# A hybrid decoder trunk on one core: the modulation vectors as row sums on VectorE, and h made one K-tile at a time

## The chip, the cores and the metric

One core of a Trainium2 chip. The metric is device time in microseconds (us) of one execution, the median over runs. Engines: TensorE (PE; its weight loads are PEld), VectorE (DVE), ScalarE (ACT), GpSimd (POOL), and SyncE (SP), on whose queue nearly all DMAs are issued.

## The reference

Two layers of a sub-layer of width 2048 over 512 tokens, batch 1. What matters here is how each layer begins and ends:

```python
c_act = jax.nn.silu(c)                                # (1, 2048)
for l in range(2):
    mod = c_act @ w_mod[l] + b_mod[l]                 # w_mod[l]: 2048 x 6144
    shift, scale, gate = jnp.split(mod, 3, axis=-1)
    h = rmsnorm(x, norm_gain[l]) * (1.0 + scale) + shift
    proj = h @ w_in[l]                                # 2048 x 7504, f32
    ...   # sparse attention with an indexer and top-k; chunked retention; SiLU gates
    x = x + gate * (y @ w_out[l])
```

`mod` is a matrix-vector product: 100 MB of `w_mod` in all, read once, for 12,288 numbers. Nothing of a layer's projection can begin before `shift` and `scale` of the first K-tile (128 of the 2048 columns) are known.

## The kernel before, in words

Everything is kept transposed: features on 128 partitions, 512 tokens along the row. There are 16 K-tiles of D = 2048. Each f32 operand of a large matmul is split into a high and a low fp32r part, and three products are summed. Weights stream through a ring of three buffers: `load_chunk` issues the DMA, `split_chunk` makes the high part on ACT (L268) and the low part on DVE (L269), `chunk_mm` issues the matmuls (L315 to L317 with weights stationary, L321 to L323 with h stationary).

**Modulation before.** A block of `w_mod` has rows of D on partitions. `mod_add` (L348, L350) multiplies it by the partition's entry of silu(c) and adds it into an accumulator on DVE. After 16 row blocks `mod_sum` (L333) sums over the partitions with matmuls against a column of ones, one per 128 columns, and `mod_put` (L338 to L344) adds bias and gain. For layer 0's shift and scale this is done in five phases of 2, 2, 4, 4, 4 K-tiles (`PH`). From the second phase on, the shift half is computed on PE instead (`mod0_pe`, L396, with `cz`), and summed in `mod0_sum` (L424). The rest (layer 0's gate, layer 1's three vectors) is done in `mod_rest`, a generator advanced at a rate per weight chunk (`MODN`).

**The start stage before.** `start()` runs with a schedule written by hand, in program order on every engine. It loads x (16 tiles) and the first blocks of `w_mod`, sums squares (L532 to L541) and makes rstd (L602, L515, L518). Then, phase by phase, it makes `shiftT` and `AT`, then h for the phase's K-tiles (`make_h0`, L550 to L556: two ACT activations and a DVE subtraction), then the matmul chunks that these K-tiles allow. Those are listed in `PLAN`: `S` is the group of keys, values and indexer keys (16 K-tiles in eight chunks, four PSUM tiles, 336 columns, evacuated by `evac_s`), and `("E", i, a, b)` is K-tiles a to b of an early part of one of eight column groups: indexer queries for i below 4 (finished later by the groups Q3), one head's q and k of the retention for i of 4 and above (finished later by the groups QK). An early part is kept in SBUF (L1191) or added to what is kept (L1206); `joined` (L1198) adds it at the end. Units of the bias table (`bias_tables`: indicators on ACT L740, matmuls L753, evacuation L756, a store) are put between chunks.

**After the start stage** the groups run in this order: Q3, VB, QK (four groups, each two heads of retention), QA, GA, GB, OUT; then layer 1. `step()` takes one chunk, and `fill` gives the pending tasks (indexer, top-k, rotary, retention, attention) a budget of 4 us of DVE work per chunk. `evac_qk` of one QK group and the retention tasks of the group before it share arena slots (A0 to A7).

The functions that the change touches, with the profile's line numbers:

Of the kernel before, what the change touches and what calls it, by code (L numbers as in the profile page):

```python
# [51 lines left out]
]  # L52
# [1229 lines left out]
```

## Time and profile before

| | |
|---|---|
| median of 3 runs | 1971.2 us (1970.82 to 1971.3) |
| profiled execution, its own time | 1972.98 us |
| its span, first to last instruction | 1971.2 us, mean granted TensorE clock 0.995 |
| busy share of PE, DVE, ACT | 98%, 65%, 42% |
| DMA | 304.44 MB, mean 154 GB/s |

How to read the lines: a group's row gives the kernel line, engine, operation, output tile <- input tiles, shapes and count, then busy us in all, the mean ns of one, and the engine's idle time just ahead of these instructions with what ended it. A timeline row gives start and duration in us, then the same names. A row of the chain gives start, duration and what ran. L515 and the like are lines of the kernel before. Matmuls overlap in a pipeline, so the distance from one start to the next is what a matmul costs TensorE, not its listed duration; an f32 matmul (L333, L396, L424, L515, L541) shows as two instructions. The granted clock is 1.00 at full speed.

### The profile page before, as it was taken

How to read it: one execution, taken by the hardware profiler on the slowest of the kernel's cores; microseconds unless marked ns; L12 is line 12 of the kernel's file. 1: busy time of each engine (PE TensorE's matmuls, PEld its weight loads, DVE VectorE, ACT ScalarE, POOL GpSimd, SP SyncE). 2: the span in 40 equal slices, each digit the busy share in tenths (PEclk: the TensorE clock that was granted, in tenths of full speed). 3: DMA queues.
4: the chain of work that ended last, by engine and by line, in shares of the span. 5: the costliest groups of instructions: out<-in, count | busy, mean ns of one | idle time of the engine just before them, and what ended most of it. 6: DMA issues, size and time to landing. Idle time of an engine off the chain costs nothing.

```text
span 1971.2 us, 25044 instructions
## 1 busy us (share of the span) xinstructions
PE 1933.8 (98%) x9384; PEld 1592.9 (81%) x9384; DVE 1271.5 (65%) x2126; ACT 822.4 (42%) x1500; POOL 3.6 (0%) x16
## 2 busy tenths in 40 slices
PE   6999999999999999999999999999999999999999
PEld 5677776788888888888889888888888888888887
DVE  5766999887658865766657459847666755233232
ACT  4554694354454642332225342234444564233111
POOL 0000000000000000000000000000000000000000
PEclk9999999999999999999999999999999999999999
DMA  9878644533334736768763222333332432333443
GB/s 330 301 246 272 231 151 145 165 101 103 96 113 141 238 113 229 258 229 299 260 204 108 86 85 75 106 101 93 97 107 86 129 118 65 96 97 118 139 139 106
DMA packets 170712, 304.44 MB, mean 154 GB/s; under 512 B 16736, under 2 KB 71008, under 8 KB 170592
## 3 DMA queue, kind: packets, MB, share of 16 engines
q1 hardware_dynamic: 170592, 302.86, 47.1%
q8 instruction: 73, 1.20, 0.2%
q14 instruction: 47, 0.39, 0.1%
HBM read 289.18 MB, written 13.63 MB: 154 GB/s over the span
## 4 chain that ended last, share of the span: by engine, by line
PE 85%; DVE 6%; ACT 4%; DMA 3%; issue 2%; SPq 0%; ACTq 0%; DVEq 0%
PE pj L315 19%; PE pj L317 19%; PE pj L316 19%; PE pj L321 5%; PE pj L323 5%; PE pj L322 5%; DVE wl L269 2%; DVE iacc L868 1%; DMA mw<-in_wmod_dram 1%; DVE m L867 1%; PE pdot L845 1%; DMA xT<-in_xt_dram 1%; PE pmod L396 1%; PE pm L333 1%; PE pdot L847 1%
## 5 line engine op out<-in xcount | busy, mean ns | idle before, releaser
L269 DVE TENSOR_TENSOR wl<-wf,wh 128x1024 fp32r<-128x1024 f32 (+2 forms) x308 | 366.1, 1189 | 440.7 <-ACT wh L268 427.7
L268 ACT ACTIVATE wh<-wf 128x1024 fp32r<-128x1024 f32 (+2 forms) x308 | 318.2, 1034 | 763.9 <-PE pj L316 552.1
L315 PE MATMUL pj<-h,wh 128*128 128x512 f32 x1280 | 504.4, 394 | 2.5 <-DVE vm L883 1.4
L316 PE MATMUL pj<-h,wh 128*128 128x512 f32 x1280 | 501.5, 392 | 0.0
L317 PE MATMUL pj<-h,wl 128*128 128x512 f32 x1280 | 501.4, 392 | 0.0
L315 PEld LDWEIGHTS pj<-h,wh 128*128 128x128 f32 x1280 | 241.6, 189 | 56.6 <-issue 3.7
L317 PEld LDWEIGHTS pj<-h,wl 128*128 128x128 f32 x1280 | 241.4, 189 | 50.6
L316 PEld LDWEIGHTS pj<-h,wh 128*128 128x128 f32 x1280 | 241.7, 189 | 48.7 <-issue 0.5
L321 PE MATMUL pj<-wh,h 128*128 128x512 f32 (+1 forms) x640 | 243.2, 380 | 3.4 <-ACT h L550 3.3
L323 PE MATMUL pj<-wh,h 128*128 128x512 f32 (+1 forms) x640 | 241.9, 379 | 1.8 <-DVE h L556 1.8
L322 PE MATMUL pj<-wl,h 128*128 128x512 f32 (+1 forms) x640 | 242.0, 378 | 0.0
L350 DVE SCALAR_TENSOR_TENSOR macc<-mw,cs,macc 128x1024 f32<-128x1024 f32 (+2 forms) x195 | 205.8, 1055 | 51.9 <-DMA mw<-in_wmod_dram 49.2
L315 PE MATMUL pj<-y,wh 128*128 128x512 f32 x512 | 199.6, 390 | 1.0 <-DVE xn L1163 1.0
L317 PE MATMUL pj<-y,wl 128*128 128x512 f32 x512 | 199.2, 389 | 0.0
L316 PE MATMUL pj<-y,wh 128*128 128x512 f32 x512 | 199.2, 389 | 0.0
L321 PEld LDWEIGHTS pj<-wh,h 128*128 128x128 f32 x640 | 121.4, 190 | 27.3 <-issue 4.3
L323 PEld LDWEIGHTS pj<-wh,h 128*128 128x128 f32 x640 | 121.2, 190 | 23.4 <-DVE h L556 2.7
L322 PEld LDWEIGHTS pj<-wl,h 128*128 128x128 f32 x640 | 121.5, 190 | 19.7 <-issue 0.8
L315 PEld LDWEIGHTS pj<-y,wh 128*128 128x128 f32 x512 | 96.1, 188 | 21.5 <-DVE xn L1163 1.4
L316 PEld LDWEIGHTS pj<-y,wh 128*128 128x128 f32 x512 | 96.1, 188 | 19.9
L317 PEld LDWEIGHTS pj<-y,wl 128*128 128x128 f32 x512 | 96.1, 188 | 19.9
L740 ACT ACTIVATE ind<-pos,pt 128x128 bf16<-128x128 f32 (+3 forms) x128 | 61.7, 558 | 0.1
(445 smaller groups left out, 2032.4 us busy)
## 6 DMA issues: line engine op xcount, KB each, us to landing
mw<-in_wmod_dram SPq DMA_DIRECT2D x192, 512.0 KB, 5.6
wf<-in_w_in_dram SPq DMA_DIRECT2D x152, 512.0 KB, 3.5
wf<-in_w_in_dram SPq DMA_DIRECT2D x148, 256.0 KB, 3.0
wf<-in_w_out_dram SPq DMA_DIRECT2D x64, 512.0 KB, 4.3
dec<-in_decay_dram SPq DMA_DIRECT2D x32, 256.0 KB, 4.0
xT<-in_xt_dram SPq DMA_DIRECT2D x16, 256.0 KB, 6.8
bias<-bias_d SPq DMA_DIRECT2D x16, 256.0 KB, 4.1
xr<-in_xt_dram SPq DMA_DIRECT2D x16, 256.0 KB, 5.5
```

What stands on the lines that cost most here:

```text
L268: act(h[:, :n], t[:, :n], AF.Copy)
L269: tt(lo[:, :n], t[:, :n], f(h[:, :n]), op=OP.subtract)
L315: mm(g.ps[n], wh[:, o:o + P], ah, start=s0, stop=False)
L316: mm(g.ps[n], wh[:, o:o + P], al, start=False, stop=False)
L317: mm(g.ps[n], wl[:, o:o + P], ah, start=False, stop=s1)
L321: mm(q, ah[:, n * P:(n + 1) * P], wh[:, o:o + g.N], start=s0, stop=False)
L322: mm(q, ah[:, n * P:(n + 1) * P], wl[:, o:o + g.N], start=False, stop=False)
L323: mm(q, al[:, n * P:(n + 1) * P], wh[:, o:o + g.N], start=False, stop=s1)
L333: mm(ps[:, j:j + 1], acc[:, j * P:(j + 1) * P], ones[:, :1], start=True, stop=True)
L350: stt(a, w, cs[:, rt:rt + 1], a, op0=OP.mult, op1=OP.add)
L396: mm(ps[32 * t:32 * t + 32, :wd], cz[:, 32 * (rt + u):32 * (rt + u) + 32], m0_tile[i][:, 2 * wd * u:2 * wd * u + wd], start=rnd == 0, stop ...
L740: act(v, pos[:, :w], AF.Sign, bias=pt[:, col:col + 1], scale=-1.0)
```

## The change

`w_mod` is laid out transposed by the host, in blocks of 128 columns of `mod` (on partitions) by 1024 rows of D. silu(c) is broadcast over the partitions once, as `cb`, by 16 matmuls against the identity and four ACT copies. Each block is one `tensor_tensor_reduce` on DVE: multiply by half of `cb` and sum along the row into one column, the second half starting from the first half's sum. `scale` is multiplied by the norm gain in the same instruction, and `mod_end` adds a prepared bias. The matmuls `mod_sum`, `mod0_sum` and `mod0_pe` are gone, with `cz`, the accumulators and the phases.

`start()` now makes h one K-tile at a time: four blocks of `w_mod` make shift and scale of a K-tile, and `make_h0` follows. A new `PLAN` lists the chunks, with some of them issued K-tile by K-tile; a modulation step (`mod_step`) is issued for every 2.0 us of matmul cost (`RMOD`), and one bias unit for every 6 us once three K-tiles are there. The plan holds 76 E K-tiles instead of 64: the early parts of the second QK group now reach K-tile 12 instead of 4, and those of the first Q3 group reach 6 instead of 8. High and low splits are issued separately, evacuations of a chunk after the modulation steps that follow it, and stores of the bias table after those. The load of the positions comes later. Beside the parts below, the diff moves the preparation of `pt` in `bias_tables` behind a `yield`, collects its stores in a queue, replaces `shiftT`, `AT` and `gateT` by `mod_col` wherever they are read, and builds `WORK` from `PLAN` (cost 1.36 per E K-tile, 1.85 per S K-tile).

```diff
-PH = [2, 2, 4, 4, 4]
-PK = [0, 2, 4, 8, 12, 16]
-PLAN = [
-    [("S", 0), ("E", 0, 0, 2), ("E", 1, 0, 2), ("E", 2, 0, 2), ("E", 3, 0, 2)],
-    [("S", 1), ("E", 4, 0, 4), ("E", 5, 0, 4), ("E", 6, 0, 4), ("E", 7, 0, 4)],
-    [("S", 2), ("S", 3), ("E", 0, 2, 8), ("E", 1, 2, 8), ("E", 2, 2, 8)],
-    [("S", 4), ("S", 5), ("E", 3, 2, 8), ("E", 4, 4, 12), ("E", 5, 4, 12)],
-    [("S", 6), ("S", 7)],
-]
-REST = [(0, 4), (0, 5), (1, 0), (1, 2), (1, 1), (1, 3), (1, 4), (1, 5)]
+PLAN = [("E", 0, 0, 2, 0), ("E", 1, 0, 2, 0), ("S", 0, 0), ("E", 0, 0, 2, 1), ("E", 1, 0, 2, 1), ("S", 0, 1),
+        ("E", 2, 0, 2), ("E", 3, 0, 2), ("E", 4, 0, 3), ("E", 5, 0, 3), ("S", 1), ("E", 6, 0, 4), ("E", 7, 0, 4),
+        ("E", 0, 2, 6), ("E", 1, 2, 6), ("S", 2), ("E", 2, 2, 8), ("E", 3, 2, 8), ("S", 3),
+        ("S", 4), ("E", 6, 4, 12), ("E", 7, 4, 12), ("S", 5), ("E", 4, 3, 12), ("E", 5, 3, 12), ("S", 6), ("S", 7)]
 NE = 8
-EARLY = [max(it[3] for p in PLAN for it in p if it[0] == "E" and it[1] == i) for i in range(NE)]
-ONPE = [False, True, True, True, True]
-NB0 = [0, 1, 1, 1, 1]
+EARLY = [max(it[3] for it in PLAN if it[0] == "E" and it[1] == i) for i in range(NE)]
+RMOD = 2.0
+RBIAS, KBIAS = 6.0, 3
+REST = [(0, 2, k) for k in range(16)] + [(1, q, k) for k in range(16) for q in (0, 1)] + [(1, 2, k) for k in range(16)]
 HVA = 2
-M0AHEAD = 7
+M0AHEAD = 8
 MX0 = 2
...
-    w = host["w_mod"]
-    mod = []
-    for p, n in enumerate(PH):
-        k = slice(P * PK[p], P * PK[p + 1])
-        mod.append(np.concatenate([w[0][:, :D][:, k], w[0][:, D:2 * D][:, k]], axis=1).ravel())
-    for l, b in REST:
-        mod.append(w[l][:, 2 * T * b:2 * T * (b + 1)].ravel())
+    seq = [(0, q, k) for k in range(KT) for q in (0, 1)] + REST
+    mod = np.stack([host["w_mod"][l][r * D // 2:(r + 1) * D // 2, q * D + P * k:q * D + P * (k + 1)].T
+                    for l, q, k in seq for r in range(2)])
     return {"xt": np.ascontiguousarray(host["x"].reshape(T, D).T), "positions": host["positions"].reshape(T),
-            "wmod": np.concatenate(mod), "w_in": host["w_in"], "w_out": host["w_out"],
...
-    cz = G("cz")
-    nc.vector.memset(cz, 0.0)
-    nc.vector.tensor_copy(cz.rearrange("p (k n) -> p k n", n=32)[:, :, 0:1], cs.unsqueeze(2))
     act(sm("dummy", 1), eps, AF.Sqrt)
+    cb = sm("cb", D)
+    for i in range(4):
+        ps = PX("pc")
+        for j in range(4):
+            n = 4 * i + j
+            mm(ps[:, j * P:(j + 1) * P], cs[:, n:n + 1].to_broadcast([P, P]), ident, start=True, stop=True)
+        act(cb[:, i * T:(i + 1) * T], ps, AF.Copy)
     gqk = [sm(f"gqk{l}", 1) for l in range(DEPTH)]
...
-    gateT = [sm(f"gate{l}", KT) for l in range(DEPTH)]
+    MD = [sm(f"md{l}", 3 * KT) for l in range(DEPTH)]
+    MB = [sm(f"mb{l}", 3 * KT) for l in range(DEPTH)]
+    for l in range(DEPTH):
+        b = MB[l][:, :2 * KT].rearrange("p (k a) -> p a k", a=2)
+        nc.vector.tensor_copy(b[:, 0], bm(l, 0, KT))
+        stt(b[:, 1], bm(l, KT, KT), 1.0, ng(l, 0, KT), op0=OP.add, op1=OP.mult)
+        nc.vector.tensor_copy(MB[l][:, 2 * KT:], bm(l, 2 * KT, KT))
+    def mod_col(l, q, k):
+        n = 2 * k + q if q < 2 else 2 * KT + k
+        return MD[l][:, n:n + 1]
...
+    def split_hi(i):
         g, ch = stream[i]
         n = g.kper * g.N
-        t = wf.pop(i)
         h = ring.tile([P, 1024], F32R, name="wh", tag="wh")
+        act(h[:, :n], wf[i][:, :n], AF.Copy)
+        whl[i] = h
+    def split_lo(i):
+        g, ch = stream[i]
+        n = g.kper * g.N
         lo = ring.tile([P, 1024], F32R, name="wl", tag="wl")
-        act(h[:, :n], t[:, :n], AF.Copy)
-        tt(lo[:, :n], t[:, :n], f(h[:, :n]), op=OP.subtract)
-        whl[i] = (h, lo)
-    def ahead(nd, ns):
+        tt(lo[:, :n], wf.pop(i)[:, :n], f(whl[i][:, :n]), op=OP.subtract)
+        whl[i] = (whl[i], lo)
+    def ahead(nd, ns, nh=0):
         while st["dma"] < min(nd, len(stream)):
             load_chunk(st["dma"])
             st["dma"] += 1
+        while st["hi"] < min(max(ns, nh), len(stream)):
+            split_hi(st["hi"])
+            st["hi"] += 1
+            if st["split"] < ns:
+                split_lo(st["split"])
+                st["split"] += 1
         while st["split"] < min(ns, len(stream)):
-            split_chunk(st["split"])
+            split_lo(st["split"])
             st["split"] += 1
...
-    def chunk_mm(i):
+    def chunk_mm(i, only=None, late=None):
         g, ch = stream[i]
-        first, last = ch == 0, ch == g.nch - 1
-        if first:
+        if g.ps is None:
             g.ps = [psum.tile([P, T], F32, name=f"pj{n}", tag=g.pool) for n in range(g.nt)]
-        wh, wl = whl.pop(i)
+        end = only is None or only == g.kper - 1
+        last = end and ch == g.nch - 1
+        wh, wl = whl.pop(i) if end else whl[i]
         for n in range(g.nt):
-            for kk in range(g.kper):
+            for kk in range(g.kper) if only is None else (only,):
                 k = g.k0 + ch * g.kper + kk
                 ah, al = g.act(k)
                 s0, s1 = k == g.k0, k == g.k1 - 1
...
-    def mod_sum(acc, n):
-        ps = PX("pm")
-        for j in range(n):
-            mm(ps[:, j:j + 1], acc[:, j * P:(j + 1) * P], ones[:, :1], start=True, stop=True)
-        return ps
...
-    def mod_add(a, w, rt):
-        if rt == 0:
-            ts(a, w, cs[:, rt:rt + 1], None, op0=OP.mult)
-        else:
-            stt(a, w, cs[:, rt:rt + 1], a, op0=OP.mult, op1=OP.add)
+    def mod_add(l, q, k, half, w):
+        dst = mod_col(l, q, k)
+        if half == 0:
+            a = mpart["t"] = sm("mp", 1, bufs=4)
         else:
+            a = dst
+        c = cb[:, half * D // 2:(half + 1) * D // 2]
+        nc.vector.tensor_tensor_reduce(w, w, c, scale=ng(l, k, 1) if q == 1 else 1.0,
+                                       scalar=mpart["t"] if half else 0.0, op0=OP.mult, op1=OP.add, accum_out=a)
+    def mod_end(l, a, n):
+        tt(MD[l][:, a:a + n], MD[l][:, a:a + n], MB[l][:, a:a + n], op=OP.add)
+    mpart = {}
+    N0 = 4 * KT
...
                 break
-            keys = [("mw", m0["mw"] % MWBUFS)] + [("HL", k) for k in range(max(PK[p], 2), KT)]
-            free = [k for k in keys if k not in m0_last or m0_last[k] in done]
+            keys = [("mw", m0["mw"] % MWBUFS)] + [("HL", k) for k in range(n // 4 + 1, KT)]
+            free = [k for k in keys if k not in m0_last or m0_last[k] < m0["add"] - 1]
             if not free:
...
+    def mod0_add():
+        n = m0["add"]
+        mod0_loads(n + 1)
+        mod_add(0, n // 2 % 2, n // 4, n % 2, m0_tile.pop(n))
+        if n % 4 == 3:
+            mod_end(0, n // 2 - 1, 2)
+        m0["add"] += 1
         mod0_loads()
-        if rnd == 3:
-            sh = pe0[p] = G("msh")
-            act(sh[:, :wd], ps[:, :wd], AF.Copy)
...
+        seq = [r + (half,) for r in REST for half in range(2)]
+                dma(tiles[j], wmod[N0 + j])
+        for j, it in enumerate(seq):
+            mod_add(*it, tiles.pop(j))
+            l, q, k, half = it
+            if k == KT - 1 and half and q:
+                mod_end(l, *((0, 2 * KT) if q == 1 else (2 * KT, KT)))
...
         yield
     def start():
         rot, bias = rot_tables(), bias_tables()
+        next(bias)
+        order = [3, 4, 4, 5]
         k = 0
         for n, m in enumerate(order):
             for _ in range(m):
                 load_x(k)
                 k += 1
+            mod0_loads(n + 1)
+        ahead(2, 0)
+        mod0_loads(8)
         ahead(3, 0)
         pss = [psum.tile([P, T], F32, name="prs", tag="pj") for _ in range(NB)]
         ssq = G("ssq")
         k = 0
         for n, m in enumerate(order):
             for _ in range(m):
                 sum_sq(k, pss, ssq)
                 k += 1
+            mod0_add()
+        r = sm("rcol", NB)
+        for j in range(NB):
+            act(r[:, j:j + 1], pss[j][:, :1], AF.Sqrt, bias=eps, scale=1.0 / D)
+        nc.vector.reciprocal(r, r)
+        state["rstd"] = bcast_col(r)
+        ahead(3, 2)
+        for l in range(DEPTH):
+            ts(gqk[l], cst[:, C_QG + l:C_QG + l + 1], cst[:, C_KG + l:C_KG + l + 1], P ** -0.5, op0=OP.mult, op1=OP.mult)
+        mod0_add()
+        next(rot)
+        ahead(5, 2)
+        st.update(have=0, t=0.0, tb=0.0, done=0)
+        hgen, xr = {}, {}
+        def get_xr(k):
+            if k < KT and k not in xr:
+                xr[k] = make_xr(k)
+        def mod_step():
+            n = m0["add"]
+            if n % 4 == 3:
+                get_xr(n // 4)
+            if n < N0:
+                mod0_add()
+            for k in list(hgen):
+                next(hgen.pop(k))
+                st["have"] = k + 1
+            if n % 4 == 3 and n < N0:
+                hgen[n // 4] = make_h0(n // 4, xr.pop(n // 4))
+                next(hgen[n // 4])
+        get_xr(0)
+        hgen[0] = make_h0(0, xr.pop(0))
+        next(hgen[0])
+        late, after = [], None
+        for i, only, kend, cost in WORK:
+            while st["have"] < kend:
+                if DEBUG:
+                    print("forced", i, st["have"], kend)
+                mod_step()
+            end = only is None or only == stream[i][0].kper - 1
+            ahead(max(st["done"] + 3, i + 1), max(st["done"] + 1, i + 1))
+            chunk_mm(i, only, late)
+            st["done"] += end
+            ns = st["done"] + 1 if end else 0
+            ahead(0, 0, ns)
+            st["t"] += cost
+            unit = False
+            if st["have"] >= KBIAS:
+                if "pos" not in flags:
+                    next(rot)
+                st["tb"] += cost
+                unit = st["tb"] >= RBIAS
+                st["tb"] -= RBIAS * unit
+            if unit:
+                next(bias)
+            while True:
+                if st["t"] >= RMOD:
+                    st["t"] -= RMOD
+                    mod_step()
+                ahead(ns + 3, ns)
+                if st["t"] < RMOD:
+                    break
+            for ev, n, ps in late:
+                ev(n, ps)
+            late.clear()
+            while stores:
+                stores.popleft()()
+            if unit:
+                next(bias)
         X.clear()
         st["i"] = NS
+        while stores:
+            stores.popleft()()
         spawn(rot)
         spawn(bias)
```

More of the change, by code (lines that the diff above doesn't have):

```diff
@@ L248, in hybrid_trunk @@
     wf, whl = {}, {}
-    st = {"dma": 0, "split": 0, "i": 0, "mod": 0.0}
+    st = {"dma": 0, "hi": 0, "split": 0, "i": 0, "mod": 0.0}
     def load_chunk(i):
@@ L560, in start @@
     def start():
-        madds = mod0_adds()
         rot, bias = rot_tables(), bias_tables()
-        mod0_loads(1)
-        next(rot)
-        n_add = [0]
-        def adds(n, upto):
-            lim = KT * min(upto + 1, len(PH))
-            while n > 0 and n_add[0] < lim:
-                next(madds)
-                n_add[0] += 1
-                n -= 1
-        order = [3, 3, 3, 3, 2, 2, 0, 0]
+        next(bias)
+        order = [3, 4, 4, 5]
         k = 0
         for n, m in enumerate(order):
-            mod0_loads(n + 1)
             for _ in range(m):
@@ L588, in start @@
         for n, m in enumerate(order):
-            adds(2, 0)
             for _ in range(m):
@@ L592, in start @@
                 k += 1
-                if k == KT:
-                    r = sm("rcol", NB)
-                    for j in range(NB):
-                        act(r[:, j:j + 1], pss[j][:, :1], AF.Sqrt, bias=eps, scale=1.0 / D)
-            if n == 5:
-                for l in range(DEPTH):
-                    ts(gqk[l], cst[:, C_QG + l:C_QG + l + 1], cst[:, C_KG + l:C_KG + l + 1], P ** -0.5,
-                       op0=OP.mult, op1=OP.mult)
-            if n == 6:
-                nc.vector.reciprocal(r, r)
-                state["rstd"] = bcast_col(r)
@@ L649, in start @@
-        for i in ids:
-            ahead(i + 6, i + 3)
-            chunk_mm(i)
+            mod0_add()
[8 more added lines that the diff above has]
+        mod0_add()
@@ L730, in bias_tables @@
         yield 1.5, False
+        pos = tab["pos"]
+        pt = sm("pt", P)
+        p4 = pos.rearrange("p (m l) -> p l m", l=4)
+        for tl in range(4):
+            ts(pt[32 * tl:32 * tl + 32, :], p4[32 * tl:32 * tl + 32, tl, :],
+               cst[32 * tl:32 * tl + 32, C_THR:C_THR + 1], None, op0=OP.subtract)
         def indicators(j, q):
@@ L1207, in more @@
                 return ev
[L1209 to L1220 removed]
+            made = {}
+            for it in PLAN:
+                only = None
+                if it[0] == "S":
+                    if ("S", it[1]) not in made:
+                        made["S", it[1]] = len(gs)
+                        gs.append((S, it[1]))
+                    ids = [made["S", it[1]]]
+                    only = it[2] if len(it) > 2 else None
+                else:
+                    _, i, a, b = it[:4]
+                    only = it[4] if len(it) > 4 else None
+                    if (i, a, b) not in made:
+                        cols = [(QI + 256 * i, 256)] if i < 4 else [(QB + P * (i - 4), P), (KB + P * (i - 4), P)]
+                        kper = next(k for k in (4, 3, 2) if (b - a) % k == 0)
+                        g = Group(W_in, cols, kper, "t", 2, hact, more(i) if a else keep(i), pool="px", name="B", kr=(a, b))
+                        made[i, a, b] = [len(gs) + ch for ch in range(g.nch)]
+                        gs += [(g, ch) for ch in range(g.nch)]
+                    ids = made[i, a, b]
+                for i in ids:
+                    g, ch = gs[i]
+                    k0 = g.k0 + ch * g.kper
+                    n = 1 if only is not None else g.kper
+                    WORK.append((i, only, k0 + (g.kper if only is None else only + 1), n * (1.85 if g is S else 1.36)))
             seq = [Group(W_in, [(QI + 512 * i, 512)], 2, "t", 4, hact,
@@ L1251, in hybrid_trunk @@
         if l == 0:
-            n0, NS = len(gs), sum(len(p) for p in CH.values())
+            n0, NS = len(gs), max(w[0] for w in WORK) + 1
     with tc.manual_schedule():
```

180 lines of the change are left out of this document (28 added, 152 removed).

## The prediction

> **What bounds the kernel now.** I read the page first, then busy time by stretches, then the chain in order of time, then the groups by shape inside the first 200 us, which the change rewrites.
>
> ```profile
> span 1971.2 us, 25044 instructions
> PE 1933.8 (98%) x9384; PEld 1592.9 (81%) x9384; DVE 1271.5 (65%) x2126; ACT 822.4 (42%) x1500; POOL 3.6 (0%) x16
> PE 85%; DVE 6%; ACT 4%; DMA 3%; issue 2%; SPq 0%; ACTq 0%; DVEq 0%
> mw<-in_wmod_dram SPq DMA_DIRECT2D x192, 512.0 KB, 5.6
> ```
>
> TensorE is the bound: 98% busy and 85% of the chain. A matmul taken off it is time, unless TensorE then waits for VectorE. The stretches show where that could be (columns: stretch; its length; busy us and instructions of PE, PEld, DVE, ACT, POOL; granted clock; DMA share; GB/s).
>
> ```profile
> 0.00:37.60 37.60, 20.26 (x88) 19.37 (x88) 21.81 (x41) 18.27 (x31) 0.20 (x4) 1.00 0.99 347
> 37.60:198.70 161.10, 156.07 (x928) 119.50 (x929) 103.84 (x176) 83.26 (x160) 1.57 (x6) 0.96 0.80 271
> 198.70:350.00 151.30, 148.50 (x800) 108.33 (x799) 144.83 (x276) 102.54 (x186) 0.00 (x0) 1.00 0.55 182
> 350.00:600.00 250.00, 247.83 (x1148) 206.01 (x1148) 187.06 (x266) 117.83 (x217) 0.00 (x0) 1.00 0.38 116
> 1800.00:1900.00 100.00, 100.00 (x443) 82.81 (x442) 28.79 (x27) 19.10 (x18) 0.00 (x0) 1.00 0.42 137
> 99.09:102.75 3.66, 3.66 (x25) 3.55 (x23) 2.13 (x3) 2.69 (x7) 0.00 (x0) 1.00 0.02 2
> 67.90:73.30 5.40, 5.40 (x28) 4.43 (x24) 5.16 (x13) 0.78 (x2) 0.00 (x0) 1.00 0.95 351
> 91.90:98.90 7.00, 7.00 (x26) 5.58 (x26) 4.54 (x10) 6.22 (x9) 0.00 (x0) 0.76 0.63 249
> 20.00:40.00 20.00, 14.74 (x62) 13.74 (x62) 14.49 (x28) 9.36 (x17) 0.00 (x0) 1.00 1.06 377
> ```
>
> Dense 512-column matmuls start every 100/443 = 0.226 us (1800 to 1900); the 336-column ones of S every 3.66/24 = 0.152 us (four n-tiles, two K-tiles, three products make 24). The second row is the start stage, in which modulation, h and the first weights go side by side. By PLAN it holds 64 E K-tiles of 6 matmuls (1.354 us each, 86.7) and 16 S K-tiles of 12 (29.3): 116 us of dense work, and 14 bias units, in 161 us. That gap is what the change attacks. VectorE is 64% busy there, and 96% in the stretch behind it.
>
> **Part 1, the matmuls removed.**
>
> ```profile
> L333 PE MATMUL pm<-cst,macc 128*128 128x1 f32 x128 | 14.7, 245 | 0.0
> L396 PE MATMUL pmod<-mw,cz 128*32 128x512 f32 x96 | 12.8, 604 | 0.0
> L396 PE MATMUL pmod<-mw,cz 128*32 128x256 f32 x32 | 2.6, 391 | 0.0
> L424 PE MATMUL pm<-cst,macc 128*128 128x1 f32 x36 | 5.5, 273 | 0.0
> L424 PE MATMUL pm<-cst,msh 128*128 128x1 f32 x28 | 3.8, 253 | 2.9 <-ACT msh L403 2.9
> 617.89 1.68 PE pm L333 x16
> 1228.92 1.68 PE pm L333 x16
> ```
>
> The chain has eight pieces of L333 from 617.89 to 1228.92, 1.68 us each, in stretches where TensorE is full: 8 x 1.68 = **-13.4**. What they did becomes the accumulator output of the new additions and two or three small VectorE adds, hidden by VectorE's slack there. The L396 and L424 rows go too, but lie inside the start stage and are counted there. The 128 later additions keep count and size (512 KB loads).
>
> **Part 2, the price of one half block.** The new instruction, a tensor_tensor_reduce of 128x1024, is not in the trace; smaller ones are (L1074).
>
> ```profile
> L350 DVE SCALAR_TENSOR_TENSOR macc<-mw,cs,macc 128x1024 f32<-128x1024 f32 x120 | 153.6, 1280 | 43.6 <-DMA mw<-in_wmod_dram 42.2
> 606.41 0.42 DVE L1074 CUSTOM_DVE_ANT_0 bias<-bias,iacc 128x256 f32<-128x256 f32 x1
> 606.75 0.08 DVE L1074 DVE_READ_ACCUMULATOR2_ANT mx<- 128x1 f32 x1
> 607.89 0.08 DVE L1074 DVE_READ_ACCUMULATOR2_ANT mx<- 128x1 f32 x1
> 608.00 0.15 DVE L1076 TENSOR_SCALAR mx<-mx 128x1 f32<-128x1 f32 x1
> 652.87 0.69 DVE L1074 CUSTOM_DVE_ANT_0 bias<-bias,iacc 128x512 f32<-128x512 f32 x1
> 653.48 0.29 DVE L1112 TENSOR_TENSOR ptl<-ptr,pth 128x128 fp32r<-128x128 f32 x1
> ```
>
> From its start to the next start it takes 0.34 us at 256 columns and 0.61 at 512, so 0.27 per 256: 1.15 at 1024. The second half reads the first half's accumulator; the trace's nearest case (607.89 to 608.00) adds 0.11. I take **1.22**; bounds 1.15 and 1.30 (duration with the accumulator read). An old 1024-wide addition lasts 1.28, so the 128 later ones change nothing.
>
> **Part 3, up to the first dense matmul.**
>
> ```profile
> 24.87 1.31 ACT L535 ACTIVATE sq<-xT 128x512 f32<-128x512 f32 x2 [1.42 <-DMA xT<-in_xt_dram]
> 30.37 2.08 PE L515 MATMUL prb<-cst,rcol 128*128 128x128 f32 x8 [0.57 <-DVE rcol L602]
> 32.48 0.60 ACT L518 ACTIVATE rstd<-prb 128x512 f32<-128x512 f32 x1 [2.38 <-PE prb L515]
> 37.67 0.65 PE L321 MATMUL pj<-wh,h 128*128 128x336 f32 x1 [3.31 <-ACT h L550]
> 198.57 0.32 PE L323 MATMUL pj<-wh,h 128*128 128x336 f32 x1
> ```
>
> The last x lands before 24.87, 7.6 us ahead of rstd, and h follows 5.2 later; the last row is the last S matmul, the stage's end. Before, all eight loads of phase 0 (4.2 MB) must land for h; now four, and x ends earlier: 2.1 MB at 377 GB/s is 5.6 us. Added in front: the broadcast of c, 16 matmuls like L515's four in 2.08 us (8.3 us) and four copies on ACT ahead of the squares. These mostly run while x is on its way, but squares that began early now queue behind them; I charge 1.4. Behind rstd stand two W splits, a fifth addition and one xr on VectorE. The positions load moves back on SP's queue; its reader now comes much later. **First dense matmul at 33.5, -4.2** (bounds -6.6 and +2).
>
> **Part 4, the start stage.** TensorE: PLAN now has 76 E K-tiles, 76 x 1.354 = 102.9, plus S 29.3, plus bias units: one per 6 us after three K-tiles, about 18 at 0.6: **143 us**. For VectorE, durations in this stretch, with 0.08 less from start to start:
>
> ```profile
> L350 DVE SCALAR_TENSOR_TENSOR macc<-mw,cs,macc 128x512 f32<-128x512 f32 x45 | 33.6, 747 | 3.6 <-DMA mw<-in_wmod_dram 2.9
> L269 DVE TENSOR_TENSOR wl<-wf,wh 128x1024 fp32r<-128x1024 f32 x11 | 13.5, 1224 | 15.4 <-ACT wh L268 15.4
> L556 DVE TENSOR_TENSOR h<-xT,h 128x512 fp32r<-128x512 f32 x14 | 9.6, 691 | 7.5 <-ACT xT L554 7.5
> L544 DVE TENSOR_TENSOR xT<-xT,rstd 128x512 f32<-128x512 f32 x14 | 9.6, 684 | 0.0
> L1206 DVE TENSOR_TENSOR part<-pj,part 128x512 f32<-128x512 f32 x12 | 8.1, 686 | 2.7 <-PE pj L317 2.7
> ```
>
> 64 additions less five made earlier: 59 x 1.22 = 72; 15 xr, 16 h, 16 part adds (eight groups of two tiles continue a part) at 0.61: 28.7; 15 small modulation adds 3.8; W splits of 24,832 columns at 1.14 per 1024: 27.6; the rest 3. **135 us**, against 104 before. Neither engine hides the other: each K-tile hands over from VectorE to ACT to VectorE to TensorE, and part adds wait for TensorE. Nearest row: h waits 7.5 us for ACT in 14 cases, 0.5 each. I charge 1.0 for each of 15 handovers: stage 158, bounds 147 (143 and one clock ramp) and 175 (below). DMA is no bound: 64 loads of w_mod (33.5 MB), x (4.2) and some 16 of weights, bias and constants by 191 us are 280 GB/s, against 347 in the first row. SP issues loads in order, so w_mod loads queue behind W loads that wait for a split; eight loads ahead are 10 us of additions against 5.6 to landing. Toward the last K-tiles h takes the buffers and three remain, 3.7 us of cover: that is in the 15.
>
> Stage end 33.5 + 158 = 191.5 against 198.7: **-7.2** with part 3 included. It also does 12 more E K-tiles (16.2) and four more bias units (2.6) that now fail to come later: **-18.8**.
>
> **Part 5, behind the stage.** Those 12 K-tiles come off the second QK group (six chunks to two), while the first Q3 group gains a chunk. This gap covered heads 0 and 1:
>
> ```profile
> 385.73 0.68 DVE L1198 TENSOR_TENSOR join<-pj,part 128x512 f32<-128x512 f32 x1
> 407.11 0.28 PE L947 MATMUL psc<-rh,rl 128*128 128x256 f32 x1
> ```
>
> The scores of the first QK group end 21 us after its last join, and the next group's evacuation reuses their arena slots. Two chunks (24 matmuls each) cover 10.9 us, plus small work. Once that cover is gone TensorE can wait some 5 to 10 us; against it, the Q3 chunk (5.4) falls into the stretch that VectorE fills at 96% and partly disappears. **+4**, bounds -4 and +12.
>
> **Sum.** The profiled execution took 1973.0 us, 1.8 more than its span. 1973.0 - 13.4 - 7.2 - 18.8 + 4 = 1937.6. The median of the runs, 1971.2, is 1.8 below that execution, so **1936**.
>
> **Rivals.** (a) *TensorE alone sets the stage*: 147 instead of 158, no wait in QK: 1936 - 11 - 4 = **1921**. For it: DVE's sum is 8 us below PE's. Against: in-order handovers.
>
> (b) *Every K-tile restarts the clock.* The stretch 91.90 to 98.90 ran 24 dense matmuls at a granted clock of 0.76 in 7.00 us; 67.90 to 73.30 ran 24 at 1.00 in 5.40. One ramp costs 1.6. With 0.5 of wait, 15 handovers cost 31.5: stage 174.5, **1952**. Before had five such handovers, after has sixteen; against it, each K-tile feeds some 8 us of matmuls, so TensorE need not run dry.
> [...]
>
> (c) *The half block is dear: slower than before.* If the accumulating form at 1024 columns, chained through a scalar, took p instead of 1.22, the stage would be 63 + 59p + 23; the 35 us gained are gone at p = 1.81, and at 2.44 the time is 1936 + 72 = **2008**. For it: the width and the chained scalar are new. Against: 0.34 and 0.61 are a straight line.
>
> (d) *The gain is given back*: VectorE, at 96% from 198.7 to 350, still decides when masks and scores are ready, and the stage also comes out at 175: 17 and 18.8 lost: **1971**.
>
> **Chances.** Forecast 0.52 (1925 to 1948), (a) 0.17, (b) 0.18, (c) 0.07, (d) 0.06. The range 1917 to 1960 holds forecast, (a) and (b), leaving out (c), (d) and edges. A difference of 0.2% (4 us) is about what measurement tells from none. Faster 0.87, same 0.05, slower 0.08.
>
> **What would show it.** The new VectorE instruction near 1.22 us from start to start, 1.8 or more for (c). First dense matmul near 33 us. The last S matmul of layer 0 near 190, with VectorE over 85% busy before it; near 180 for (a). Granted clock 0.96 or better from there back to 34; clearly lower for (b). No pm, pmod rows. A TensorE gap of some us between the second and third QK group of layer 0. The second layer is shorter only by its two pm sums. Wrong would be: dense work in the start stage held up by loads of w_mod, or a stage past 200.

## The result, and the profile after

The changed kernel takes **1938.4 us** (median, 1936.18 to 1940.4) against 1971.25 for the kernel before beside it: ratio 0.9832, 95% interval 0.9815 to 0.9849, 32.8 us faster. The forecast was 1936. The profiled execution took 1936.18 us with a span of 1934.4.

The page's first lines and the chain of the kernel after, to hold against those of before:

```profile
span 1934.4 us, 24571 instructions
PE 1896.9 (98%) x9096; PEld 1567.9 (81%) x9096; DVE 1293.3 (67%) x2305; ACT 819.0 (42%) x1501; POOL 5.4 (0%) x16
PE 76%; DVE 13%; ACT 4%; DMA 4%; issue 3%; SPq 0%; DVEq 0%; ACTq 0%
```

TensorE has 36.9 us less work (1933.8 to 1896.9) and is still 98% busy: the span follows it. VectorE's part of the chain doubled, from 6% to 13%. Where that lies is seen in the stretches of after (start stage, the stretch behind it, then the start stage in two parts; columns as before):

```profile
32.70:196.80 164.10, 155.04 (x876) 121.73 (x877) 144.49 (x240) 95.22 (x187) 3.42 (x6) 0.95 0.89 291
196.80:350.00 153.20, 151.17 (x783) 115.80 (x782) 149.48 (x308) 92.46 (x161) 0.00 (x0) 1.00 0.61 196
32.70:143.90 111.20, 102.16 (x550) 79.85 (x551) 99.01 (x162) 59.37 (x116) 0.00 (x0) 0.93 0.89 295
143.90:196.80 52.90, 52.88 (x327) 41.88 (x327) 45.48 (x79) 35.84 (x71) 3.42 (x6) 1.00 0.89 282
```

VectorE is 88% busy in the stage (64% before), TensorE 94%. In the first part TensorE sits idle for 9.0 us and runs at a mean clock of 0.93; in the second it is full, with VectorE still 86% busy. The same stage in the groups of VectorE, by shape:

```profile
L355 DVE CUSTOM_DVE_ANT_0 mw<-mw,cb,mp 128x1024 f32<-128x1024 f32 x33 | 43.1, 1307 | 1.6 <-DMA mw<-in_wmod_dram 1.6
L355 DVE CUSTOM_DVE_ANT_0 mw<-mw,cb 128x1024 f32<-128x1024 f32 x18 | 21.9, 1219 | 0.9 <-DMA mw<-in_wmod_dram 0.9
L355 DVE CUSTOM_DVE_ANT_0 mw<-mw,cb,cst 128x1024 f32<-128x1024 f32 x15 | 19.2, 1280 | 2.1 <-DMA mw<-in_wmod_dram 2.1
L276 DVE TENSOR_TENSOR wl<-wf,wh 128x1024 fp32r<-128x1024 f32 x10 | 12.2, 1232 | 4.3 <-ACT wh L269 4.3
L1178 DVE TENSOR_TENSOR part<-pj,part 128x512 f32<-128x512 f32 x16 | 10.4, 684 | 1.9 <-PE pj L331 1.9
```

The 66 row sums wait for data 4.6 us in all. No group with pm or pmod is left. Four rows of after's timeline show the stage's ends and its longest wait, between the second and the third row (start, duration):

```profile
32.77 0.80 PE L329 MATMUL pj<-h,wh 128*128 128x512 f32 x1 [5.37 <-ACT h L510]
...
134.20 0.39 PE L331 MATMUL pj<-h,wl 128*128 128x512 f32 x1
137.22 0.80 PE L329 MATMUL pj<-h,wh 128*128 128x512 f32 x1 [2.63 <-ACT h L510]
...
196.75 0.32 PE L337 MATMUL pj<-wh,h 128*128 128x336 f32 x1
```

So the stage runs from 32.8 to 196.8: 164.0 us, where 158 was forecast. The traces place the rest; times are starts of the first such instruction, in us, with the distance to the column before in brackets:

| | first dense matmul | last S matmul | first QK evacuation | QA evacuation | OUT addition | last OUT of layer 0 | span |
|---|---|---|---|---|---|---|---|
| before | 37.7 | 198.6 (160.9) | 381.7 (183.1) | 580.8 (199.1) | 897.5 (316.7) | 1036.5 (139.1) | 1971.2 (934.7) |
| after | 32.8 | 196.8 (164.0) | 379.6 (182.8) | 558.8 (179.3) | 867.9 (309.0) | 1001.9 (134.0) | 1934.4 (932.5) |
| gained up to here | 4.9 | 1.8 | 2.1 | 22.0 | 29.6 | 34.6 | 36.8 |

Over half of the gain comes in the QK groups, where the early K-tiles are missing, and most of the rest behind QA, where of the change's parts only the matmuls of `mod_sum` had lain.

### The profile page after: what moved, and what is told of

Same layout as the page of the kernel before. It is cut to its first block, busy times and chain, and to the rows that moved or that the text cites. A ratio compares the mean times of both kernels' runs of the same rounds, so it can differ in the third digit from the quotient of the medians.

```text
span 1934.4 us, 24571 instructions
## 1 busy us (share of the span) xinstructions
PE 1896.9 (98%) x9096; PEld 1567.9 (81%) x9096; DVE 1293.3 (67%) x2305; ACT 819.0 (42%) x1501; POOL 5.4 (0%) x16
## 4 chain that ended last, share of the span: by engine, by line
PE 76%; DVE 13%; ACT 4%; DMA 4%; issue 3%; SPq 0%; DVEq 0%; ACTq 0%
PE pj L329 19%; PE pj L330 19%; PE pj L331 19%; PE pj L335 3%; PE pj L337 3%; PE pj L336 3%; DVE wl L276 3%; DVE mw L355 2%; DVE iacc L840 2%; DMA mw<-in_wmod_dram 2%; DVE m L839 1%; DMA wf<-in_w_in_dram 1%; DVE iacc L825 1%; PE ptr L167 1%; PE prs L501 1%
## 5 line engine op out<-in xcount | busy, mean ns | idle before, releaser
L276 DVE TENSOR_TENSOR wl<-wf,wh 128x1024 fp32r<-128x1024 f32 (+3 forms) x309 | 366.2, 1186 | 473.1 <-ACT wh L269 462.2
L269 ACT ACTIVATE wh<-wf 128x1024 fp32r<-128x1024 f32 (+3 forms) x309 | 318.0, 1031 | 732.9 <-PE pj L330 513.6
L355 DVE CUSTOM_DVE_ANT_0 mw<-mw,cb,mp 128x1024 f32<-128x1024 f32 x96 | 124.6, 1299 | 12.7 <-DMA mw<-in_wmod_dram 12.0
L329 PEld LDWEIGHTS pj<-y,wh 128*128 128x128 f32 x512 | 96.1, 188 | 19.9
L331 PEld LDWEIGHTS pj<-y,wl 128*128 128x128 f32 x512 | 96.1, 188 | 19.9
L355 DVE CUSTOM_DVE_ANT_0 mw<-mw,cb 128x1024 f32<-128x1024 f32 x64 | 78.0, 1220 | 11.3 <-DMA mw<-in_wmod_dram 9.5
```

The costliest lines, as they stand in the source:

```text
L269: act(h[:, :n], wf[i][:, :n], AF.Copy)
L276: tt(lo[:, :n], wf.pop(i)[:, :n], f(whl[i][:, :n]), op=OP.subtract)
L329: mm(g.ps[n], wh[:, o:o + P], ah, start=s0, stop=False)
L331: mm(g.ps[n], wl[:, o:o + P], ah, start=False, stop=s1)
L355: nc.vector.tensor_tensor_reduce(w, w, c, scale=ng(l, k, 1) if q == 1 else 1.0, scalar=mpart["t"] if half else 0.0, op0=OP.mult, op1=OP.ad ...
```

## Experiments

Theory 1: the amount of work on VectorE sets the length of the start stage. The rivals (TensorE's sum, the order of issue, the waits at single places) stand in the expectations. Times of the stage below are from the first dense to the last S matmul.

**Half of each row sum left out (e2_half_sum).** In `mod_add`:

```diff
+        if l == 0 and q < 2:
+            w, c = w[:, :T], c[:, :T]
```

> The changed kernel, but layer 0's shift and scale sum only 512 of each half block's 1024 columns (the other half of the sum is left out); the loads stay whole. Theory 1, VectorE's work sets the start stage: each of the 59 additions of the stage gets about 0.58 us shorter (34 us of VectorE's 144), the stage falls from 164 to TensorE's own 144 to 150, the time by 14 to 20 us, to about 1921. Theory 2, the handover of each K-tile and the clock restarts set it: only the last addition of each K-tile lies in the handover, some 0 to 9 us less, 1930 to 1938. Theory 3, the arrival of w_mod sets it: no change, 1938.

1922.3 us, ratio 0.9753 [0.9738, 0.9768]: 16 us below after. Its start stage:

```profile
31.90:180.70 148.80, 148.12 (x875) 119.02 (x876) 113.55 (x238) 95.40 (x187) 2.23 (x6) 0.98 0.96 322
```

With 31 us less on VectorE the stage falls by 15.2 and stops where TensorE is full (148.12 of 148.8). So the other 15 us of after's stage come from VectorE, and a stage at TensorE's sum alone, rival (a), is what one would have with VectorE out of the way: 1922 against the 1921 worked out for it.

**A second, short sum behind each row sum (e3_extra_256).**

```diff
+        if l == 0 and q < 2:
+            nc.vector.tensor_tensor_reduce(w[:, :256], w[:, :256], c[:, :256], scale=1.0, scalar=0.0,
+                                           op0=OP.mult, op1=OP.add, accum_out=sm("mx2", 1, bufs=4))
```

> The changed kernel with a second, 256-column multiply-and-sum behind each of layer 0's shift and scale additions (its result is not used, but it alters 256 of the block's columns after they were summed). It puts 59 x 0.34 = 20 us more on VectorE in the start stage. Theory 1 (VectorE's work sets the stage): 18 to 20 us slower, about 1957. Theory 2 (handovers): VectorE has 20 us of idle time in the stage that can take it, 0 to 6 us slower. Theory 3 (loads): no change.

1955.6 us, 0.9921 [0.9906, 0.9936]: 17.2 more than after. The stage and the added group:

```profile
33.40:214.50 181.10, 158.24 (x875) 122.27 (x876) 168.42 (x359) 94.91 (x186) 2.42 (x6) 0.95 0.81 263
...
L358 DVE CUSTOM_DVE_ANT_0 mw<-mw,cb 128x256 f32<-128x256 f32 x59 | 25.1, 425 | 2.0
```

VectorE does 24 us more, the stage is 17.2 longer: added work on VectorE is paid at 0.7 of its size, and rival (c)'s mechanism, a dearer half block, is real, only its price was not.

**Row sums issued earlier and later (e7_rmod17, e8_rmod23).** `RMOD` 1.7 and 2.3 instead of 2.0.

> The changed kernel with a modulation step per 1.7 us of matmul cost instead of 2.0: h comes earlier against the W splits and part additions. Theory 1: VectorE's sum is the same, the waits only move from h to the splits; within 4 us of 1938. Theory 2: the three long waits for h (at 59 to 61, 96 to 98 and 134 to 139 us) and the clock restarts behind two of them go, 6 to 10 us faster, about 1930. Theory 3: no change.

1953.1 us, 0.9912 [0.9895, 0.9929]: 14.7 slower, where both theories expected little or a gain. Two views, the stage and the waits:

```profile
32.80:209.00 176.20, 156.34 (x875) 121.83 (x876) 154.77 (x256) 95.75 (x182) 0.00 (x0) 0.94 0.88 296
```

```profile
PE pj L329 <- ACT wh L269: 8.4, 2, 5.6
```

The mistake was to think that the pace moves only the order. Layer 0's 64th sum starts at 163.9 instead of 171.9, and behind it VectorE goes on with sums of the later modulation: 16 of them start before the last S matmul, where after has 7. They belong to `mod_rest`, since `mod_step` issues none after the 64th; what set them among the start stage's instructions on VectorE's queue was not traced. VectorE has 10.3 us more and the stage is 12.2 longer. TensorE's longest wait in it, 5.6 us up to 171.3, is for a high part of weights, which on ScalarE's queue stands behind the activation that makes h, and that one waits 5.9 us for VectorE's row sums. Another 5.0 us come between the stage and the first QK evacuation.

> The changed kernel with a modulation step per 2.3 us of matmul cost instead of 2.0. With 1.7 the time was 15 us longer, TensorE waiting for weights instead of h. Theory 1 (VectorE's sum sets the stage, 2.0 is near the balance of its two uses): later h, more forced steps, 0 to 8 us slower, about 1942. Rival (each step earlier costs, each step later gains): faster, about 1928.

1942.4 us, 0.9856 [0.9841, 0.987]: 3.9 slower, within what was expected, and at the edge of what can be told. Later sums take no work from VectorE's 144 us and make h later: TensorE's idle time in the stage is 11.7 us instead of 9.0. The stage itself is only 0.9 longer; 2.6 come between it and the first QK evacuation and 1.1 in the QK part.

**The xr products on GpSimd (e6_xr_pool).** In `make_xr`:

```diff
-        tt(X[k], X[k], state["rstd"], op=OP.mult)
+        (tt if k < 1 else nc.gpsimd.tensor_tensor)(X[k], X[k], state["rstd"], op=OP.mult)
```

> The changed kernel with 15 of the 16 products x * rstd on GpSimd instead of VectorE. Theory 1: VectorE loses 15 x 0.61 = 9 us of the stage, about 1930, provided that GpSimd makes one in less than the 10 us that a K-tile takes and does not slow VectorE. Theory 2: these products are made ahead of the last addition and are not in the handover, no change, 1938. Theory 3: no change.

1946.0 us, 0.9874 [0.9859, 0.9888]: 7.6 slower, a miss for theory 1 as put there. Ten us of work left VectorE, and others grew. Groups of this run, in its first 250 us, and one in its stage:

```profile
L504 POOL TENSOR_TENSOR xT<-xT,rstd 128x512 f32<-128x512 f32 x15 | 26.6, 1806 | 28.0 <-ACT rstd L478 28.0
L516 DVE TENSOR_TENSOR h<-hv,h 128x512 fp32r<-128x512 f32 x2 | 3.5, 1737 | 0.0
L504 DVE TENSOR_TENSOR xT<-xT,rstd 128x512 f32<-128x512 f32 x1 | 1.7, 1737 | 0.0
```

```profile
L355 DVE CUSTOM_DVE_ANT_0 mw<-mw,cb,mp 128x1024 f32<-128x1024 f32 x33 | 46.1, 1398 | 2.8 <-DMA mw<-in_wmod_dram 2.6
```

The 15 products need only rstd, so GpSimd makes all of them in a row, from 28.5 to 55.1, and not one per K-tile. VectorE's first two subtractions and its one product of that size take 1737 ns instead of some 690 (its 14 later subtractions take 690), and the chained row sums 1398 on the mean of the whole stage instead of 1307. The first of those hit sit in front of the first h: the first dense matmul starts at 36.7 instead of 32.8. Why they are longer, no trace shows. The products themselves take 1806 ns on the mean on GpSimd, against 686 on VectorE in after.

**The two halves of the change apart (e1_rest_only, e4_short_plan, e5_before_long_plan).** First, the kernel before with only the later modulation (`mod_rest`) as row sums, its stage untouched:

```diff
-REST = [(0, 4), (0, 5), (1, 0), (1, 2), (1, 1), (1, 3), (1, 4), (1, 5)]
+REST = [(0, 2, k) for k in range(16)] + [(1, q, k) for k in range(16) for q in (0, 1)] + [(1, 2, k) for k in range(16)]
...
-            mod_add(acc, tiles.pop(j), rt)
+            nc.vector.tensor_tensor_reduce(w, w, cb[half], scale=ng(l, k, 1) if q == 1 else 1.0,
+                                           scalar=mpart["t"] if half else 0.0, op0=OP.mult, op1=OP.add, accum_out=a)
```

> The kernel before with one part of the change alone: layer 0's gate and layer 1's three vectors as row sums (transposed layout, tensor_tensor_reduce); the start stage keeps its phases. The broadcast of c is made when these additions begin (16 matmuls, some 3.5 us of TensorE, since the accumulators' memory has to be free). Theory 1 (a matmul off TensorE is time there): 8 x 1.68 = 13.4 less, 3.5 more, about 10 us faster than before, 1961. Rival (the gain behind the start stage comes from the other parts, the eight sums are hidden or given back): within 4 us of 1971.

1961.8 us, 0.9957 [0.9941, 0.9974]: 8.8 less than before. Its stage (161.3) and QK part (199.8) stand as before; QA to OUT falls by 5.6, OUT by 5.0. So a good quarter of the gain needs nothing of the new stage.

Then the kernel after without the 16 early K-tiles that the second QK group gained:

```diff
-        ("S", 4), ("E", 6, 4, 12), ("E", 7, 4, 12), ("S", 5), ("E", 4, 3, 12), ("E", 5, 3, 12), ("S", 6), ("S", 7)]
+        ("S", 4), ("S", 5), ("E", 4, 3, 12), ("E", 5, 3, 12), ("S", 6), ("S", 7)]
```

> The changed kernel without the 16 early K-tiles 4 to 12 of the second QK group in PLAN; that group does them itself, as before (six chunks instead of two). Theory 1 (VectorE's work sets the start stage): the stage loses 4 splits and 4 part additions, some 7 us, while QK gets 21.8 us longer and loses its 2 us wait: 11 to 14 us slower, about 1951. Rival (TensorE's work sets the stage): 21.7 us shorter there, 21.8 longer behind, no change, 1938.

1943.6 us, 0.9866 [0.9851, 0.9881], 5.2 more than after: between the two. The stage:

```profile
33.00:178.80 145.80, 130.69 (x732) 103.99 (x732) 129.67 (x215) 79.80 (x158) 0.00 (x0) 0.94 0.87 286
```

The stage is 18.2 shorter, the stretch from there to the first QK evacuation 4.0 longer (the shorter stage holds four bias units fewer), the QK part 21.7 longer. Taking work from both engines (TensorE 24.3, VectorE 14.8) frees most of what comes back later; the longer plan is worth the small rest. And the same 16 K-tiles given to the kernel before, as the last items of its fourth phase:

```diff
+      ("E", 6, 4, 12), ("E", 7, 4, 12)],
```

> The kernel before with the same 16 early K-tiles added to its fourth phase. Theory 1: its phases end in waits for the modulation sums and its stage is set by TensorE's order, so 21.7 us are added to the stage and 21.8 taken from QK: within 4 us of 1971, the plan alone brings nothing. Rival (the plan alone brings the gain, by filling idle time): 10 to 18 us faster, about 1957.

1969.2 us, 0.9996 [0.9987, 1.0005]: no change. Its stage:

```profile
37.40:224.00 186.60, 181.63 (x1071) 138.63 (x1072) 112.89 (x185) 96.53 (x181) 1.86 (x6) 0.96 0.76 255
```

TensorE is at 181.63 of 186.6: the stage grew by 25.7, QK fell by 21.5. Moving early K-tiles about gains nothing by itself. In after, a part of them fills time in which TensorE would stand idle: 15.1 us of the stage without them, 9.1 with them.

**Covering the longest wait (e9_reordered).** By now I read the first part of the stage (to 144 us) as paced by VectorE, with its wait for h at 134 to 137 and the slow clock behind it worth 5 to 8 us, and the second part as TensorE's. The plan's last items, cut so that TensorE has K-tiles below 9 to work on at that point:

```diff
-        ("S", 4), ("E", 6, 4, 12), ("E", 7, 4, 12), ("S", 5), ("E", 4, 3, 12), ("E", 5, 3, 12), ("S", 6), ("S", 7)]
+        ("E", 6, 4, 8), ("E", 7, 4, 8), ("S", 4), ("E", 4, 3, 9), ("E", 5, 3, 9), ("S", 5),
+        ("E", 6, 8, 12), ("E", 7, 8, 12), ("E", 4, 9, 12), ("E", 5, 9, 12), ("S", 6), ("S", 7)]
```

> The kernel after with the order of PLAN's last lines changed and nothing left out: the early parts E6, E7 (K-tiles 4 to 12) and E4, E5 (3 to 12) are each cut in two, so that TensorE has matmuls on K-tiles below 9 to do where it now waits for h at 134 to 144 us. Eight more part additions on VectorE (8 x 0.61 = 4.9 us). Theory 1 as refined (up to about 144 us VectorE sets the pace of h, with TensorE waiting and restarting its clock between 134 and 144, some 5 + 3 us; behind that TensorE is full): these waits are covered, the stage ends 4 to 8 us earlier, about 1932. Rival (VectorE's sum alone sets the stage): 4.9 us more of VectorE's work, about 1943. If neither, the wait only moves to another K-tile, within 3 us of the kernel after (1938).

1945.0 us, 0.9874 [0.9858, 0.9891]: 6.5 slower, the rival's side. Two stretches and a timeline of this run:

```profile
32.70:200.70 168.00, 154.08 (x876) 119.35 (x877) 147.16 (x242) 94.82 (x187) 3.14 (x6) 0.98 0.86 280
133.00:145.00 12.00, 10.13 (x70) 7.66 (x69) 10.84 (x19) 5.06 (x9) 0.00 (x0) 1.00 0.84 254
```

```profile
182.35 0.39 PE L332 MATMUL pj<-h,wl 128*128 128x512 f32 x1
185.47 0.50 PE L330 MATMUL pj<-h,wh 128*128 128x512 f32 x1 [2.73 <-DVE part L1179]
```

The wait and the slow clock at 134 did go: the second row stands at full clock, where after shows 0.72 in the same stretch. But TensorE now waits at 139.6, 161.4 and 182.4 to 185.5, for weights and for part additions, and the stage is 4.0 longer, near the 4.9 us of additions put on VectorE; 2.7 more come between the stage and the first QK evacuation. My reading of the second part fell: TensorE is full there only as long as VectorE has the slack that after leaves it.

**More and fewer bias units in the stage (e10_bias45, e11_bias90).** They cost VectorE nothing (it is busy for 143.2 and 143.4 us in these stages, 144.5 in after's), so of the two engines they change TensorE's work alone (`RBIAS` 4.5 and 9 instead of 6).

> The kernel after with a bias unit for every 4.5 us of matmul cost instead of every 6, nothing left out: about 25 of the 32 units fall into the start stage instead of 19. One costs TensorE some 0.65 to 0.8 us from the matmul before it to the matmul behind it, so 4 to 5 us of TensorE's work move in front of the stage's end, at no cost to VectorE. Theory 1 (VectorE's sum sets the stage; TensorE waits some 9 us of it): the stage grows by less than half of that and the time falls 2 to 5 us, about 1935. Rival (TensorE is full behind 144 us and its waits before that are not where the units fall): the stage grows by all of it, no change, 1938. Rival (the indicators, four activations of some 0.4 to 0.6 us for each unit, stand ahead of h on ACT's queue): slower by 3 us or more.

> The same the other way: a bias unit for every 9 us, nothing left out, so about 13 in the start stage instead of 19. Theory 1: the stage shrinks by less than half of the 4 us taken out, and the units cost their full price later: 2 to 4 us slower, about 1941. Rival (TensorE sets the stage's end): no change, 1938. Rival (the indicators on ACT delay h): faster by 2 us or more.

1940.3 us, 0.9847 [0.9833, 0.9861], and 1942.6 us, 0.986 [0.9845, 0.9876]; after is 0.9832 [0.9815, 0.9849]. The first can't be told from after, the second is 4 us slower, at the edge of what can be told. Their stages, 4.5 first:

```profile
32.40:202.40 170.00, 161.30 (x947) 124.62 (x948) 143.24 (x232) 110.61 (x212) 0.73 (x2) 0.95 0.87 288
```

```profile
32.80:195.10 162.30, 147.83 (x791) 116.51 (x792) 143.42 (x240) 78.86 (x147) 1.07 (x2) 0.98 0.87 285
```

With fewer units (12 instead of 19) TensorE is busy for 7.2 us less, 4.6 of them because the two slow stretches behind the start are gone, and the stage shrinks by only 1.6, as theory 1 says. With more (25), TensorE is busy for 6.3 us more and the stage grows by 6.0: all of it, against theory 1's less than half. The traces show nothing won back behind it: the profiled execution is 5.0 us longer than after's, though the medians are only 1.8 apart. The stage of after is thus a corner: work added to either engine is paid (0.7 of VectorE's, all of TensorE's), work taken from TensorE alone is repaid in part, work taken from VectorE is repaid until TensorE is full. Neither sum alone is the bound.

## Why the prediction was right, point by point

The total was right to 2.4 us, partly because two terms were wrong by five us each way.

**Part 1**, the matmuls of the later sums: -13.4 forecast; the three distances behind QA's evacuation give 7.6 + 5.0 + 2.2 = 14.8. Right. The experiment with that part alone gave 8.8 by the medians and 11.5 by the spans; there the broadcast of c stands in the middle of the run, at 373 to 380 us, and takes 3.9 us of TensorE.

**Part 2**, the half block: in after's timeline a chained sum, a scaled one, what comes behind, and ahead of them a split of weights:

```profile
130.61 1.23 DVE L276 TENSOR_TENSOR wl<-wf,wh 128x1024 fp32r<-128x1024 f32 x1 [1.85 <-ACT wh L269]
131.76 1.28 DVE L355 CUSTOM_DVE_ANT_0 mw<-mw,cb,mp 128x1024 f32<-128x1024 f32 x1
132.96 0.08 DVE L355 DVE_READ_ACCUMULATOR2_ANT md<- 128x1 f32 x1
132.96 1.28 DVE L355 CUSTOM_DVE_ANT_0 mw<-mw,cb,cst 128x1024 f32<-128x1024 f32 x1
134.17 0.09 DVE L355 DVE_READ_ACCUMULATOR2_ANT mp<- 128x1 f32 x1
134.17 0.69 DVE L504 TENSOR_TENSOR xT<-xT,rstd 128x512 f32<-128x512 f32 x1
134.77 1.34 DVE L355 CUSTOM_DVE_ANT_0 mw<-mw,cb,mp 128x1024 f32<-128x1024 f32 x1
136.04 0.08 DVE L355 DVE_READ_ACCUMULATOR2_ANT md<- 128x1 f32 x1
```

131.76 to 132.96 and 132.96 to 134.17 are 1.20 and 1.21; one that is both chained and scaled takes 1.27 (134.77 to 136.04). 1.22 was right, and the straight line from 256 and 512 columns, which gave 1.15, holds to 1024: a sum neither chained nor scaled takes 1.14 (30.04 to 31.18). Rival (c) is out.

**Part 3**, the first dense matmul: 33.5 forecast, 32.77 measured. Right.

**Part 4**, the stage: 158 forecast, 164.0 measured, within the bounds but 6 too low: the step that failed. The forecast was TensorE's sum, 143, and 15 handovers of 1.0. The 143 was the term that was too low. With VectorE out of the way (the first experiment) the same matmuls take 148.8 us with 0.7 idle. The 19 bias units come to some 0.7 us each there, an estimate (148.8 less 132.2 of dense work, the idle time and the start at half clock), where 18 at 0.6 were counted. The start at half clock was left out of the sum; in after:

```profile
32.77:38.03 5.26, 4.51 (x10) 3.23 (x11) 5.26 (x9) 0.60 (x1) 0.00 (x0) 0.50 1.05 388
```

At half clock the 512-column matmuls start 0.43 apart (34.91, 35.33), behind it 0.23 (38.19, 38.42). So the busy 4.51 us are worth about half, and this costs some 2.3 us, an estimate. The forecast's lower bound counted 4 us for one clock ramp (147 less 143), which no row shows. The kernel before begins its stage in the same way: its first matmuls of 336 columns start 0.28 apart (39.18, 39.46) up to 41.7 and 0.15 apart from 42.0 on, though its profile shows a clock of 1.00 there.

The remaining 15 us of after's stage are what the handovers were charged, but they are not 15 handovers. The trace shows 9 us of idle time at a few places and two more stretches at half clock:

```profile
99.47:102.88 3.41, 3.41 (x9) 2.63 (x8) 2.40 (x3) 2.42 (x6) 0.00 (x0) 0.50 0.85 280
102.90:137.00 34.10, 31.41 (x199) 24.77 (x197) 30.92 (x52) 18.39 (x36) 0.00 (x0) 1.00 0.88 278
137.02:143.84 6.82, 5.84 (x13) 4.29 (x14) 6.24 (x10) 1.90 (x3) 0.00 (x0) 0.50 0.80 275
```

With matmuls 0.43 apart again (99.92, 100.35), half clock costs about half of the busy time there, some 1.7 and 2.9 us. Each stands behind a longer gap: TensorE starts nothing between 96.00 and 98.23 (a split of weights is late), nor between 134.20 and 137.22 (h of one K-tile is late). VectorE's rows above show why h was late: from 130.61 on it was working through its queue without a pause, the split, the row sums, the xr product and the sums again. Just before, it stood idle for 1.85 us, because that split, ahead of the sums in its queue, waited for ScalarE. So rival (b)'s ramp exists, at the start and twice behind it, not fifteen times (the kernel before has it at the start and four times: 3.41 us at 0.50 from 62.4, 93.1, 137.5 and 185.3). Both long gaps go back to VectorE: the first ends with a low part of weights, the second with an activation that had waited 3.8 us for its sums.

What the 15 us depend on is VectorE's amount of work, which added nothing to the forecast's sum: they go with 31 us less of it and become 32 with 24 us more. That amount, 135, was itself too low by 9: 66 row sums fall into the stage, the 59 of layer 0 that were counted (the added sums of the second experiment are 59 too) and seven of the later modulation that were not, 8.5 us by 1.22. That 15 times 1.0 gave the right size for waits of another kind was luck. The two tries to remove a single wait or thin out TensorE show that no one wait is worth its length.

**The moved work and Part 5**: -18.8 and +4, together -14.8. The two distances from the last S matmul to QA's evacuation give -0.3 and -19.9: -20.2. This is the other error, 5.4. The 16 K-tiles taken from the second QK group are 21.7 us, of which 19.9 appear. The QK part, before and then after, and the stretch of after from the second group's evacuation to the third's:

```profile
381.70:580.80 199.10, 198.37 (x924) 165.75 (x923) 147.36 (x204) 99.05 (x167) 0.00 (x0) 1.00 0.33 101
379.60:558.80 179.20, 176.67 (x823) 146.44 (x822) 172.15 (x255) 94.92 (x163) 0.00 (x0) 1.00 0.55 178
397.00:446.50 49.50, 49.50 (x230) 41.15 (x231) 48.27 (x74) 27.55 (x50) 0.00 (x0) 1.00 0.53 162
```

TensorE is idle for 2.5 us in the QK part of after, against 0.7 before: that is the difference. Where the wait was feared, between the second and third group, there is none at all. VectorE is 98% busy there (48.27 of 49.5), so the cover is thin, but it holds. The other half of Part 5 held too: the added Q3 chunk (5.4 us) and five bias units fewer (some 4) leave the first Q3 to QK distance as it was, 182.8 against 183.1, in a stretch that VectorE fills at 98%.

**The sum.** Against the forecast the stage's end came 5.3 later, the work behind it 5.4 shorter and the later sums 1.4 better: 1937.6 + 5.3 - 5.4 - 1.4 = 1936.1, the profiled execution's 1936.18. The forecast's bounds for single terms held; that their errors cancelled was luck. Rival (d) did not come about: the stretch behind the stage stayed as long as it was, and the stage came out at 164, not 175.

## What to carry to other kernels

Work moved from a full engine to a half-idle one gained at once here where the stage had slack on the second (14.8 us from the later sums); where both came near 90% busy (94% and 88%), waits between the engines' queues left TensorE idle for 9 of 164 us, and the one visible wait that was covered came back elsewhere. Price such a stage by both sums plus some idle time, count also the later work that falls into it and a start at half clock, and test the price from both sides (a bit more and a bit less work on each engine) before believing one bound. Split a change into its parts: here 8.8 of 32.8 us came from the simplest one, and 5 from the longer plan, which gains nothing without the rest.
